# Tile starts, one moved recombination unit, one moved split and two re-divided copies in a two-layer encoder

## The chip, the cores and the metric

The kernel runs on one core of one Trainium2 chip. The metric is device time in microseconds of one execution. A core has five engines that run side by side, each with its own queue of instructions in a fixed order: TensorE (PE in the profile; PEld is its loading of stationary operands), VectorE (DVE), ScalarE (ACT), GpSimd (POOL) and SyncE (SP), which here issues the loads of the weights. They wait for each other through semaphores. SBUF is the on-chip memory (128 partitions), PSUM the memory into which TensorE accumulates.

## The reference

An encoder trunk of two layers in float32, for one sequence of 256 tokens with 2048 features. Each sub-layer is normalised in front and added to its input:

```
h = x
h = h + mixer_a(rms_norm(h, g0), w_a, w_ao, ...)   # grouped-query attention: 16 heads, 4 key/value heads
h = h + ffn(rms_norm(h, g1), w_up, conv, w_down)   # gated, a width-3 depthwise convolution between
h = h + mixer_b(rms_norm(h, g2), w_b, w_bo, bias)  # 3 groups of 8 heads: windows (128,1), (512,4), (2048,16)
h = h + ffn(rms_norm(h, g3), w_up, conv, w_down)
out = rms_norm(h, g4)
```

The FFN's inner width is 5632, computed in 11 pairs of 512 columns. Mixer B's attention output has 3072 features, so its output projection w_bo contracts 3072 rows, six chunks of 512.

## The kernel before

**Arithmetic.** Every projection in float32 is made of three matmuls in a reduced format: an operand x is split in a high part xh and the rest xl, a weight in wh and wl, and xh·wh, xh·wl and xl·wh are added in PSUM (L126 to L128). The weights come from memory as raw tiles of 128 x 2 x 512 floats (512 KB). ScalarE makes wh from raw (L138; in the units L173), VectorE makes wl = raw - wh (L139; L174), with four buffers of each.

**Feeds and units.** `feed` is one chunk (512 rows of contraction) for one block of 512 output columns and both halves of the tokens: 24 matmuls, which need two wh. `fast_unit` does one chunk for two column blocks with a seven-product scheme: 42 matmuls where two feeds would take 48, on seven weight tiles, some of which are sums of raw tiles (VectorE, L172). It needs recombined stationary operands: s and sx in mixer A's output projection, kTh, kTl, qTh, qTl in mixer B's; these are tiles that had another use before. Its products lie in eight accumulators of PSUM; after the last unit `fold` brings the shared ones together on VectorE (L193 to L203).

**The order of the work.** `pair` runs a list of feeds and units for two column blocks. Beside the matmuls run Python generators whose steps are taken between the matmuls of a feed or a unit (`step`): the bringing over of results to the next stage, the fold, the attention's arithmetic. So the order in which a step is issued is written out by the code, while a scheduler puts each engine's instructions in a final order, with wh and wl given a priority of 60 places ahead. In the end each engine works its list strictly in order.

**The border between two stages.** When the two accumulators of a block of 512 columns are complete, VectorE adds them to h (L452), ScalarE takes the sum of squares (L359), and `late_transpose` turns the block for the next projection: two transposes of 32 x 32 blocks on VectorE (L369) into quad, then 16 copies of 32 x 256 elements into wide, the even ones on GpSimd (L390) and the odd ones on ScalarE (L388), in two halves, each followed by a `yield`; then four `put`, which scale and split into xh and xl of the next stage (ScalarE L323, VectorE L326). For the last block (n=3) the copies are divided over three engines: GpSimd by `quad_move` (L373), ScalarE (L418), VectorE (L421). The FFN that follows takes its chunks in order, so the block n=2 is its third chunk.

**Mixer B.** The projection of values and gates runs while probabilities are turned and placed in the wide tiles kTh, kTl, qTh, qTl (n = 0 to 3; `place` in the value stage), for the two halves of the heads one after the other (hf = 0, 1). Each placing is `quad_move`: 16 copies on GpSimd (L373). Small matmuls with the values (L1265, ps<-wide,v) use them as soon as they are there. The output projection then does column blocks 0 and 1 with feeds alone, and blocks 2 and 3 with units for chunks 0 and 2 and feeds for chunks 1, 3, 4, 5.

**Memory.** Tiles come from pools in the order of their first use in the code, so the byte at which a tile begins in a partition depends on what was taken before it.

Of the kernel before, what the change touches and what calls it, by code (L numbers as in the profile page):

```python
# [7 lines left out]
F32 = mybir.dt.float32  # L8
F32R = mybir.dt.float32r
# [4 lines left out]
P = 128  # L14
# [16 lines left out]
def tile_encoder(ctx: ExitStack, tc: tile.TileContext, x, xT, w_a, w_ao, q_gain, k_gain, w_b, w_bo,  # L31
# [7 lines left out]
    small = ctx.enter_context(tc.tile_pool(name="small", bufs=2))  # L39
# [10 lines left out]
    nc.scalar.activation(act0, nhalf, AF.Copy)  # L50
    nc.gpsimd.dma_start(ident, ident_c)
    h = hpool.tile([P, 2, D], F32, name="h")

    uid = [0]

    def nm(s):
        uid[0] += 1
        return f"{s}_{uid[0]}"
# [30 lines left out]
    def drain(keep=0):  # L89
        while len(pending) > keep or beside:  # L90
            step(True)
            if len(pending) > keep:
                step()
# [111 lines left out]
    def pair(wd, ns, lhs, order, spot, folds, post, hurry=0, ready=None):  # L205
        (a2, a4), (a3, a8) = new_acc(), new_acc()
        acc, begun = {2: a2, 3: a3, 4: a4, 8: a8}, set()
        sides = [a2, a4], [a3, a8]
        fasts = [kg for kg, side in order if side is None]

        added = []

        def finish(side):
            add_residual(sides[side], ns[side])
            added.append(side)

        def closing():
            yield from fold(acc, *ns, *folds())
            for side in range(2 if post else 0):
                yield  # L220
                while side not in added:
                    yield
                post(ns[side])

        for i, (kg, side) in enumerate(order):
            while ready is not None and kg not in ready:
                step()
            if side is None:
                if kg == fasts[0]:
                    while beside:  # L230
                        step(True)
                    while ready is not None and "u" not in ready:
                        step()
                    acc.update({q: ps_tile() for q in (1, 5, 6, 7)})
                later = {s for _, s in order[i + 1:]}
                end = [q for q, s in ((1, None), (5, None), (6, None), (7, None), (2, 0), (4, 0), (3, 1))
                       if not later & {None, s}]
                fast_unit(acc, lhs[-1 - kg], wd[ns[0], kg], wd[ns[1], kg], begun, end, spot)
                if kg == fasts[-1]:
                    beside.append(closing())  # L240
                    if 0 not in later:
                        finish(0)
                continue
            mine = ((2, 4), (3, 8))[side]
            end = not any(s in (side, None) for _, s in order[i + 1:])
            feed(sides[side], lhs, kg, wd[ns[side], kg], not begun.issuperset(mine), end,
                 begun=[m for m in range(2) if mine[m] in begun])
            begun.update(mine)
            for _ in range(hurry):
                if pending:  # L250
                    step()
            if end:
                finish(side)
# [108 lines left out]
    def quad_tile(pool, tag, bufs=1):  # L362
        return pool.tile([P, 4, 8, 32], F32, tag=tag, name=nm("quad"), bufs=bufs)

    def wide_tile(pool, tag, bufs=1):
        return pool.tile([P, 8, P], F32, tag=tag, name=nm("wide"), bufs=bufs)
# [4 lines left out]
    def quad_move(o, quad, qcs=QC):  # L371
        for q, c in qcs:
            nc.gpsimd.tensor_copy(o[32 * c:32 * c + 32, :, 32 * q:32 * q + 32],  # L373
                                  quad[32 * q:32 * q + 32, c])
# [8 lines left out]
    def quad_place(o, quad, i0, i1):  # L383
        for i in range(i0, i1):
            q, c = QC[i]
            dst, src = o[32 * c:32 * c + 32, :, 32 * q:32 * q + 32], quad[32 * q:32 * q + 32, c]
            if i % 2:
                nc.scalar.activation(dst, src, AF.Copy)  # L388
            else:
                nc.gpsimd.tensor_copy(dst, src)  # L390

    def late_transpose(hT, n, g, pool, tag, new_quad):
        def put(kt, src):
            hT[kt] = new_hT(kt)
            split_scaled(*hT[kt][:2], src, gain[:, g, kt:kt + 1])

        yield
        if n < 3:
            quad = new_quad()
            for m in range(2):  # L400
                quad_T(quad, slice(m, 8, 2), h[:, m, n * 512:(n + 1) * 512])
            yield
            o = wide_tile(pool, tag)
            for i in range(0, 16, 8):
                quad_place(o, quad, i, i + 8)
                yield
            for j in range(4):
                put(4 * n + j, o[:, 2 * j:2 * j + 2].rearrange("p m c -> p (m c)"))
            return
        space, quad_tag, wide_tag = next_space[0]  # L410
        src = h[:, :, n * 512:(n + 1) * 512]
        quad, o = quad_tile(space, *quad_tag), wide_tile(space, *wide_tag)
        for m in range(2):
            quad_T(quad, slice(m, 8, 2), src[:, m])
        quad_move(o, quad, BY_POOL)
        yield
        for q, c in BY_ACT:
            nc.scalar.activation(o[32 * c:32 * c + 32, :, 32 * q:32 * q + 32], quad[32 * q:32 * q + 32, c], AF.Copy)  # L418
        for q, c in BY_DVE:
            rows, cols = slice(32 * q, 32 * q + 32), slice(32 * c, 32 * c + 32)  # L420
            nc.vector.transpose(o[cols, :, rows].rearrange("p (j m) t -> p j m t", m=2),  # L421
                                src[rows].rearrange("p m (j c) -> p j m c", c=P)[:, :, :, cols])
        yield
        yield
        for j in range(4):
            if j % 2 == 0:
                yield
            put(4 * n + j, o[:, 2 * j:2 * j + 2].rearrange("p m c -> p (m c)"))
# [54 lines left out]
    def ffn(l, hT, ss_in, cw, g_next, last, side=None):  # L483
        with tc.tile_pool(name=nm("fpool"), bufs=1) as fp:
            junk = junk_of(fp)
            next_space[0] = fp, ("quad", 2), ("cv", 1)
            drain(1)
            step()
            rstd = finish_rstd(ss_in)
# [148 lines left out]
            for hf, (p0, p1) in enumerate(HALVES):  # L638
                slots = {}
                ready.clear()  # L640
                new_us()
                fast = (1, 2)
                last_value = None
                for p in range(p0, p1):
                    k0 = 4 * (p - p0)
                    slots.update(new_slots(range(k0, k0 + 4)))
                    cg = fp.tile([P, 4, NT], F32, tag="cg", name=nm("cg"))
                    cv = fp.tile([P, 4, NT], F32, tag="cv", name=nm("cv"))
# [97 lines left out]
                both = {kg: [(kg, 0), (kg, 1)] for kg in rest}  # L746
                f0, f1 = ([(kg, None)] for kg in fast)
# [16 lines left out]
    def out_proj(w, slots, kgs, late, g_next, junk, pool, tag, new_quad, cuts=(), units=None):  # L764
        hTn, ss = {}, new_ss()

        def post(n):
            sumsq_cols(ss, n, junk)
            start(late_transpose(hTn, n, g_next, pool, tag, new_quad))

        def done(accs, n):
            add_residual(accs, n)
            post(n)

        if units:
            fast, own, tmp, spot, folds, raws = units
            done(project2(w, 0, 1, slots, kgs, late, lambda a: done(a, 0), None, cuts,
                          [lambda kg=kg: recombined(kg, slots, own, tmp) for kg in fast]), 1)
            extra[0] = raws
            both = {kg: [(kg, 0), (kg, 1)] for kg in sorted(kgs) if kg not in fast}  # L780
            (k0, k1, *ks), (f0, f1) = list(both), fast
            pair(w, (2, 3), slots, both[k0] + [(f0, None)] + both[k1] + [(f1, None)] + sum((both[k] for k in ks), []),
                 spot, folds, post)
            extra[0] = None
            drain(1)
            return hTn, ss
        done(project2(w, 0, 1, slots, kgs, late, lambda a: done(a, 0), None, cuts), 1)
        for n in (2, 3):
            done(project(w, n, slots, kgs), n)
        return hTn, ss  # L790
# [330 lines left out]
    def mixer_b(hT, ss_in):  # L1121
        with tc.tile_pool(name="bpool", bufs=1) as bp:
# [5 lines left out]
            slots = {}  # L1128
# [25 lines left out]
            for hf in range(2):  # L1154
# [61 lines left out]
                def value_stage(hf=hf, probs=probs, e=e, vs=vs):  # L1216
# [16 lines left out]

                    def place(quad, n):
                        o = wide_tile(bp, ("kTh", "kTl", "qTh", "qTl")[n])
                        quad_move(o, quad)
                        if n < 2:
                            for i in range(2):
                                turned[0, 2 * n + i] = o[:, 4 * i:4 * i + 4].rearrange("p x c -> p (x c)")
                        else:  # L1240
                            for i in range(4):
                                turned[n - 1, i] = o[:, 2 * i:2 * i + 2].rearrange("p x c -> p (x c)")
# [31 lines left out]
                    for n in range(2):  # L1274
                        quad = new_quad()
# [5 lines left out]
                    for n in (2, 3):  # L1281
                        i = 2 * (n - 2)
                        quad = new_quad()
# [138 lines left out]
```

## Time and profile before

| what | value |
| --- | --- |
| median of three runs | 2248.28 us (2247.81 to 2248.5) |
| profiled execution | 2248.33 us |
| its span | 2246.6 us |
| mean granted TensorE clock | 0.999 of full |
| TensorE busy | 2228.4 us (99%) |
| VectorE busy | 1718.7 us (77%) |
| ScalarE busy | 1313.3 us (58%) |
| GpSimd busy | 796.7 us (35%) |
| instructions | 28737 |

The span runs from the first to the last instruction of the profiled execution. In the views shown below a row of the timeline gives the start in us from the span's start, how long it lasted, the engine, the line of the code, the operation, the tile written and the tiles read, the shape, the number of like instructions in the row, and in brackets for how long the engine sat idle before it and what ended that. A row of the groups gives the count after the shape, then the total busy time and the mean ns of one. Matmuls overlap: one of 512 columns lasts about 390 ns, but the next starts some 227 ns after it. A tile's name stands without its buffer's number.

### The profile page before, as it was taken

What the parts mean: (1) busy time and instruction counts of PE and PEld (TensorE: products, weight loads), DVE (VectorE), ACT (ScalarE), POOL (GpSimd) and SP (SyncE); (2) the same over time, 40 slices, a digit from 0 to 9 for tenths busy, and PEclk for the clock granted to TensorE, in tenths of its full rate; (3) what the DMA queues carried; (4) which work ended last, traced back from release to release, by engine and by line L of the source; (5) the groups of instructions that cost most, each with busy time, mean ns of one, the idle gap of its engine ahead of it and who ended that gap; (6) DMA issues with size and microseconds to landing.
All of it is one profiled execution on the core that took longest, in us unless ns stands there. A gap on an engine that the chain in (4) does not pass through costs nothing.

```text
span 2246.6 us, 28737 instructions
## 1 busy us (share of the span) xinstructions
PE 2228.4 (99%) x10005; PEld 1842.9 (82%) x10005; DVE 1718.7 (77%) x2211; ACT 1313.3 (58%) x1842; POOL 796.7 (35%) x1051
## 2 busy tenths in 40 slices
PE   9999999999999999999999999999999999999998
PEld 7888888888888888888888888878888888888887
DVE  6877667778876788878877878686777798677795
ACT  7676655656545666755454554566665655465663
POOL 2343255661005563220062008013766500256601
PEclk9999999999999999999999999999999999999999
DMA  8665666565666565666666555556656566665653
GB/s 302 194 218 181 217 188 198 192 193 187 201 208 193 192 193 180 202 198 198 186 192 192 182 185 181 190 177 211 195 182 205 187 206 200 194 194 190 216 198 131
DMA packets 126178, 439.58 MB, mean 196 GB/s; under 512 B 14408, under 2 KB 18248, under 8 KB 126032
## 3 DMA queue, kind: packets, MB, share of 16 engines
q1 hardware_dynamic: 123056, 429.05, 59.0%
q0 software_dynamic: 2688, 8.39, 1.5%
q8 instruction: 78, 1.28, 0.2%
q14 instruction: 68, 0.56, 0.1%
q10 hardware_dynamic: 288, 0.30, 0.0%
HBM read 432.34 MB, written 5.34 MB: 195 GB/s over the span
## 4 chain that ended last, share of the span: by engine, by line
PE 83%; DVE 5%; POOL 1%; ACT 1%; issue 1%; DMA 1%; SPq 0%; POOLq 0%; DVEq 0%; ACTq 0%
PE acc L128 26%; PE acc L127 26%; PE acc L126 26%; DVE wl L174 1%; DVE wl L139 1%; PE ps L180 1%; PE ps L181 1%; PE ps L179 1%; PE acc L180 1%; PE acc L181 1%; PE acc L179 1%; POOL wide L390 1%; DVE cv L537 1%; POOL wide L373 1%; DVE u L172 0%
## 5 line engine op out<-in xcount | busy, mean ns | idle before, releaser
L139 DVE TENSOR_TENSOR wl<-raw,wh 128x1024 fp32r<-128x1024 f32 (+1 forms) x748 | 936.2, 1258 | 366.6 <-ACT wh L138 362.5
L138 ACT ACTIVATE wh<-raw 128x1024 fp32r<-128x1024 f32 (+1 forms) x748 | 782.8, 1050 | 658.4 <-PE acc L128 586.8
L126 PE MATMUL acc<-wh,xh 128*128 128x512 f32 x2176 | 848.3, 390 | 0.5 <-ACT wh L138 0.5
L127 PE MATMUL acc<-wl,xh 128*128 128x512 f32 x2176 | 847.3, 389 | 0.3 <-DVE wl L139 0.2
L128 PE MATMUL acc<-wh,xh 128*128 128x512 f32 x2176 | 847.2, 389 | 0.0
L550 POOL COPY u<-quad 32x256 f32<-32x256 f32 x672 | 483.1, 719 | 338.5 <-DVE quad L369 312.3
L128 PEld LDWEIGHTS acc<-wh,xh 128*128 128x128 f32 x2176 | 408.4, 188 | 85.0
L127 PEld LDWEIGHTS acc<-wl,xh 128*128 128x128 f32 x2176 | 408.7, 188 | 84.3 <-DVE wl L139 1.3
L126 PEld LDWEIGHTS acc<-wh,xh 128*128 128x128 f32 x2176 | 408.7, 188 | 84.3 <-ACT wh L138 0.9
L126 PE MATMUL acc<-wh,a 128*128 128x512 f32 x720 | 280.9, 390 | 0.0
L128 PE MATMUL acc<-wh,a 128*128 128x512 f32 x720 | 280.3, 390 | 0.0
L127 PE MATMUL acc<-wl,a 128*128 128x512 f32 x720 | 280.3, 389 | 0.0
L373 POOL COPY wide<-quad 32x256 f32<-32x256 f32 x165 | 111.1, 673 | 175.2 <-DVE quad L369 167.5
L128 PEld LDWEIGHTS acc<-wh,a 128*128 128x128 f32 x720 | 135.1, 188 | 28.4 <-DVE a L320 0.2
L126 PEld LDWEIGHTS acc<-wh,a 128*128 128x128 f32 x720 | 135.2, 188 | 27.8
L127 PEld LDWEIGHTS acc<-wl,a 128*128 128x128 f32 x720 | 135.2, 188 | 27.8
L390 POOL COPY wide<-quad 32x256 f32<-32x256 f32 x72 | 44.3, 615 | 207.1 <-DVE quad L369 193.2
L480 ACT ACTIVATE stg<-acc,rstd 128x512 f32<-128x512 f32 x122 | 82.9, 686 | 33.3 <-PE acc L128 33.2
L567 POOL TENSOR_TENSOR cv<-cg,cv 128x1024 f32<-128x1024 f32 x18 | 58.2, 3231 | 105.2 <-DVE cv L537 105.2
L173 ACT ACTIVATE wh<-raw 128x1024 fp32r<-128x1024 f32 x56 | 59.4, 1061 | 49.2 <-PE acc L128 44.3
L537 DVE SCALAR_TENSOR_TENSOR cg<-u,cw,cg 128x256 f32<-128x256 f32 x176 | 82.3, 511 | 4.5 <-ACT cg L529 4.5
L520 POOL MEMSET u<- 128x4 f32 x12 | 1.0, 107 | 231.8 <-DVE wl L174 211.9
(284 smaller groups left out, 2004.7 us busy)
## 6 DMA issues: line engine op xcount, KB each, us to landing
raw<-in_w_up_dram SPq DMA_DIRECT2D x352, 512.0 KB, 4.5
raw<-in_w_down_dram SPq DMA_DIRECT2D x176, 512.0 KB, 4.5
raw<-in_w_b_dram SPq DMA_DIRECT2D x144, 512.0 KB, 4.4
raw<-in_w_bo_dram SPq DMA_DIRECT2D x48, 512.0 KB, 4.2
raw<-in_w_a_dram SPq DMA_DIRECT2D x40, 512.0 KB, 4.7
raw<-in_w_ao_dram SPq DMA_DIRECT2D x32, 512.0 KB, 4.8
raw<-in_w_a_dram SPq DMA_DIRECT2D x16, 256.0 KB, 5.7
there<-quad POOLq DMA_DIRECT2D x6, 512.0 KB, 4.6
```

The lines of the kernel that those rows point to most:

```text
L126: nc.tensor.matmul(accs[m], xh, wh[:, j, :], start=st, stop=False)
L127: nc.tensor.matmul(accs[m], xh, wl[:, j, :], start=False, stop=False)
L128: nc.tensor.matmul(accs[m], xl, wh[:, j, :], start=False, stop=sp)
L138: nc.scalar.activation(wh[:, c], r[:, c], AF.Copy)
L139: nc.vector.tensor_tensor(wl[:, c], r[:, c], wh[:, c].bitcast(F32), ALU.subtract)
L173: nc.scalar.activation(wh, r, AF.Copy)
L373: nc.gpsimd.tensor_copy(o[32 * c:32 * c + 32, :, 32 * q:32 * q + 32], quad[32 * q:32 * q + 32, c])
L390: nc.gpsimd.tensor_copy(dst, src)
L480: nc.scalar.activation(o[:, m, :], accs[m], AF.Copy, scale=rstd[:, m:m + 1])
L537: nc.vector.scalar_tensor_tensor(cj, halves(flat[:, j, o:o + NT])[:, ::-1], tap(n, j, i), cj, ALU.mult, ALU.add)
L550: nc.gpsimd.tensor_copy(o, src)
L567: made.append(eng.tensor_tensor(cv, cg, cv, ALU.mult).ins)
```

## The change

There are four edits.

1. A tile of 32 bytes per partition, `space`, that nothing uses, is taken before the later pools; and in `ffn` the tiles quad (two buffers), cv and sx (two buffers) are taken when the pool opens instead of at their first use. Both move the bytes at which tiles begin.
2. In `late_transpose`, for the blocks n < 3, one more `yield` stands between the copies and the four `put`: the splits are issued one step later.
3. In mixer B's output projection, the order list of column blocks 2 and 3: each unit comes one chunk (two feeds, 48 matmuls) later. Before it was chunk 1, unit of chunk 0, chunk 3, unit of chunk 2, chunks 4 and 5; now it is chunks 1 and 3, unit of 0, chunk 4, unit of 2, chunk 5. The loads that SP issues follow that order.
4. In mixer B's `place`, for the second half of the heads and n = 2 and 3, `quad_place` stands in place of `quad_move`: 8 of the 16 copies go to ScalarE.

The number of matmuls is the same; GpSimd has 16 copies less, ScalarE 16 more.

```diff
@@ -50,6 +50,7 @@
     h = hpool.tile([P, 2, D], F32, name="h")
+    small.tile([P, 8], F32, name="space", bufs=1)
@@ -404,6 +405,7 @@
             for i in range(0, 16, 8):
                 quad_place(o, quad, i, i + 8)
                 yield
+            yield
             for j in range(4):
                 put(4 * n + j, o[:, 2 * j:2 * j + 2].rearrange("p m c -> p (m c)"))
             return
@@ -484,6 +486,9 @@
             next_space[0] = fp, ("quad", 2), ("cv", 1)
+            quad_tile(fp, "quad", 2)
+            wide_tile(fp, "cv")
+            fp.tile([P, 6, 2, P], F32R, tag="sx", name=nm("sx"), bufs=2)
             drain(1)
@@ -778,8 +783,8 @@
             both = {kg: [(kg, 0), (kg, 1)] for kg in sorted(kgs) if kg not in fast}
-            (k0, k1, *ks), (f0, f1) = list(both), fast
-            pair(w, (2, 3), slots, both[k0] + [(f0, None)] + both[k1] + [(f1, None)] + sum((both[k] for k in ks), []),
+            (k0, k1, k2, k3), (f0, f1) = both, fast
+            pair(w, (2, 3), slots, both[k0] + both[k1] + [(f0, None)] + both[k2] + [(f1, None)] + both[k3],
                  spot, folds, post)
@@ -1233,7 +1238,10 @@
                         o = wide_tile(bp, ("kTh", "kTl", "qTh", "qTl")[n])
-                        quad_move(o, quad)
+                        if hf == 1 and n > 1:
+                            quad_place(o, quad, 0, 16)
+                        else:
+                            quad_move(o, quad)
```

What that does to the engines' lists shows at three places. The rows name line, operation, tile written and tiles read, with buffer numbers; the lines after the change are one or two higher than before for the same code. First, ScalarE in mixer B's output projection, where the splits of block 1 (xh<-wide) meet the first unit's weights (L173 before, L174 after). Before:

```order
L173 ACTIVATE wh_12939<-raw_12928 128x1024
L388 ACTIVATE wide_12859<-quad_12840 32x8x32 x6
L173 ACTIVATE wh_12949<-raw_12930 128x1024
L388 ACTIVATE wide_12859<-quad_12840 32x8x32 x2
L323 ACTIVATE xh_12912<-wide_12859,gain 128x256
L323 ACTIVATE xh_12915<-wide_12859,gain 128x256
L323 ACTIVATE xh_12918<-wide_12859,gain 128x256
L173 ACTIVATE wh_12959<-raw_12932 128x1024
```

And after, the same copies and splits with weights of feeds (L139) among and behind them:

```order
L139 ACTIVATE wh_12920<-raw_12916 128x1024
L389 ACTIVATE wide_12863<-quad_12844 32x8x32 x6
L139 ACTIVATE wh_12948<-raw_12918 128x1024
L389 ACTIVATE wide_12863<-quad_12844 32x8x32 x2
L324 ACTIVATE xh_12936<-wide_12863,gain 128x256
L324 ACTIVATE xh_12939<-wide_12863,gain 128x256
L324 ACTIVATE xh_12942<-wide_12863,gain 128x256
L139 ACTIVATE wh_12968<-raw_12964 128x1024
L324 ACTIVATE xh_12945<-wide_12863,gain 128x256
L139 ACTIVATE wh_12984<-raw_12966 128x1024
L174 ACTIVATE wh_13015<-raw_13004 128x1024
```

The unit's weights have moved behind the splits and behind the weights of feeds. Second, GpSimd from the second half of the heads in mixer B on. Before:

```order
L373 COPY wide_11854<-quad_11845 32x8x32 x16
L373 COPY wide_11896<-quad_11887 32x8x32 x16
L373 COPY wide_12106<-quad_12061 32x8x32 x16
L373 COPY wide_12228<-quad_12183 32x8x32 x16
L390 COPY wide_12745<-quad_12726 32x8x32 x8
```

After:

```order
L374 COPY wide_11858<-quad_11849 32x8x32 x16
L374 COPY wide_11900<-quad_11891 32x8x32 x16
L391 COPY wide_12110<-quad_12065 32x8x32 x8
L391 COPY wide_12232<-quad_12187 32x8x32 x8
L391 COPY wide_12749<-quad_12730 32x8x32 x8
```

The third and the fourth tile keep eight copies on GpSimd; the other eight of each stand on ScalarE's list (L389). Third, VectorE ahead of the second FFN, where block 2's accumulators are added to h (L452 before, L454 after) and turned (L369, L370). Before, the fold is far ahead of it:

```order
L139 TENSOR_TENSOR wl_13274<-raw_13253,wh_13273 128x1024
L203 TENSOR_TENSOR h<-h,fold_13184 128x512
L139 TENSOR_TENSOR wl_13296<-raw_13291,wh_13295 128x1024
L139 TENSOR_TENSOR wl_13319<-raw_13293,wh_13318 128x1024
L139 TENSOR_TENSOR wl_13420<-raw_13415,wh_13419 128x1024
L452 TENSOR_TENSOR h<-acc_12816,h 128x512
L452 TENSOR_TENSOR h<-acc_12817,h 128x512
L369 STREAM_TRANSPOSE quad_13315<-h 128x16x32 x2
L139 TENSOR_TENSOR wl_13436<-raw_13417,wh_13435 128x1024
```

After:

```order
L195 TENSOR_TENSOR fold_13261<-ps_13003,fold_13260 128x512
L197 TENSOR_TENSOR fold_13261<-ps_13001,fold_13260 128x512
L140 TENSOR_TENSOR wl_13427<-raw_13422,wh_13426 128x1024
L454 TENSOR_TENSOR h<-acc_12808,h 128x512
L454 TENSOR_TENSOR h<-acc_12809,h 128x512
L198 TENSOR_TENSOR fold_13260<-ps_13001,fold_13261 128x512
L200 TENSOR_TENSOR h<-h,fold_13260 128x512
L201 TENSOR_TENSOR h<-h,fold_13261 128x512
L370 STREAM_TRANSPOSE quad_13341<-h 128x16x32 x2
L140 TENSOR_TENSOR wl_13443<-raw_13424,wh_13442 128x1024
```

Three adds of the fold now stand between the adds to h and the transposes.

## The prediction

> **What bounds the kernel now.** I read the page first, then TensorE's waits, then the matmuls one by one around each wait.
>
> ```profile
> span 2246.6 us, 28737 instructions
> PE 2228.4 (99%) x10005; PEld 1842.9 (82%) x10005; DVE 1718.7 (77%) x2211; ACT 1313.3 (58%) x1842; POOL 796.7 (35%) x1051
> PEclk9999999999999999999999999999999999999999
> ```
>
> TensorE is busy 99% of the span at full clock, so a change gains only where TensorE waits or where its matmuls are set further apart than they need be. The other engines matter through the moment at which they hand an operand over. The waits (total us, times, longest):
>
> ```profile
> PE ps L180 <- DVE wl L174: 2.2, 5, 0.7
> PE ps L335 <- DVE qTl L320: 1.9, 1, 1.9
> PE ps L1265 <- POOL wide L373: 1.7, 2, 1.2
> ```
>
> Two of these stand where the code changes: the probability tiles of mixer B (L1265) and the unit's weights (L180). The profiled execution took 2248.33 us, 1.7 more than its span and within 0.05 of the median (2248.28), so I sum against 2248.33. A measurement of this kernel can tell about 0.2%, 4.5 us, from no change: the bounds are 2243.8 and 2252.8.
>
> **Part 1: the starts of the operands.** The built programs show where each SBUF tile begins. Before, wh, wl, xh, a, s and c begin 64 bytes past a multiple of 128; sx begins at 0 and kTh, kTl, qTh, qTl at 32. Afterwards all of these are at 64. Inside one unit of mixer A's output projection both cases stand side by side:
>
> ```profile
> 902.35 0.40 PE L179 MATMUL ps<-wh,sx 128*128 128x512 f32 x1
> ...
> 905.15 0.39 PE L179 MATMUL acc<-wh,s 128*128 128x512 f32 x1
> ...
> 906.54 0.39 PE L179 MATMUL ps<-wh,s 128*128 128x512 f32 x1
> ...
> 910.62 0.40 PE L179 MATMUL acc<-wh,sx 128*128 128x512 f32 x1
> ```
>
> From 902.35 to 905.15 twelve matmuls with sx start, one every 233.3 ns; from 906.54 to 910.62 eighteen with s, one every 226.7. Same weights, same unit, nothing waited for: 6.6 ns apart. The groups by form show the same difference over the whole span (mean ns in the middle):
>
> ```profile
> L179 PE MATMUL ps<-wh,s 128*128 128x512 f32 x72 | 28.0, 390 | 0.0
> L179 PE MATMUL ps<-wh,sx 128*128 128x512 f32 x24 | 9.5, 396 | 0.0
> L127 PE MATMUL acc<-wl,sx 128*128 128x512 f32 x48 | 19.0, 396 | 0.0
> L127 PE MATMUL acc<-wl,c 128*128 128x512 f32 x16 | 6.3, 395 | 0.0
> L181 PE MATMUL ps<-wh,kTl 128*128 128x512 f32 x6 | 2.4, 395 | 0.0
> ```
>
> There are 360 matmuls with sx in all such groups: 360 x 6.6 ns = 2.4 us. The neighbours that overlap them (48 with c and 72 with s, at about half the excess) give 0.4, and 48 with kT or qT at 5 to 6 ns 0.3. Some 80 groups of mixer B's small attention products, whose operands also begin at 32 beside ones at 64, should give about 0.9; their rows have no twin at equal starts, so 0.9 is an estimate by the same excess per matmul that overlaps one of another start. I take 4.0. Ends: 0, if the start is not the cause, and 5.0, if the attention products gain twice that.
>
> Trainium skill, "SBUF — State Buffer", section "Who interferes with whom": TensorE has one read port for the moving and an independent one for the stationary operand, and never waits on anyone. By that rule where the operands start can cost nothing, and this term would be 0. The spacing above speaks against it as far as a difference in start can be told from a difference in tile; that is the first rival.
>
> **Part 2: two probability tiles moved by ScalarE too.** For the second half of the heads, tiles n=2 and 3 get 8 copies on GpSimd and 8 on ScalarE where GpSimd made 16.
>
> ```profile
> 1390.25 0.39 PE L128 MATMUL acc<-wh,a 128*128 128x512 f32 x1
> 1391.85 0.82 PE L1265 MATMUL ps<-wide,v 128*128 128x128 f32 x5 [1.22 <-POOL wide L373]
> ```
> ```profile
> 1378.03 24.52 POOL L373 COPY wide<-quad 32x256 f32<-32x256 f32 x32 [2.90 <-DVE quad L369]
> ```
> ```profile
> L388 ACT ACTIVATE wide<-quad x72: 413/416/419, 213.4 to 1525.5; 32x256 f32<-32x256 f32 x72
> ```
> ```profile
> L390 POOL COPY wide<-quad x72: 392/396/1302, 212.8 to 1526.1; 32x256 f32<-32x256 f32 x72
> ```
> ```profile
> 1381.11 1.06 ACT L138 ACTIVATE wh<-raw 128x1024 fp32r<-128x1024 f32 x1 [1.65 <-PE acc L128]
> ```
>
> GpSimd needs 24.52 us for 32 copies, 12.3 a tile, and TensorE comes 1.2 us too early for the first and 0.5 for the second. With half the copies a GpSimd share is about 6.1 us, and ScalarE's 8 x 0.416 = 3.3 run beside it: the tile is ready some 5 to 6 us sooner, far more than 1.2. Gain: both L1265 waits, 1.7, and the restart behind each, 0.15 (1391.85 - 1390.25 - 0.23 = 1.37 lost for a wait of 1.22): 2.0. Ends: 0, if ScalarE's share comes late, and 2.0, since no more is lost there. What ScalarE's 16 copies push back are the wh copies of the projection that runs meanwhile. Each feeds 12 matmuls, 2.7 us, and there are four buffers, so a wh is wanted 3 x 2.7 = 8.2 us after its buffer is freed; ScalarE idles for that buffer (1.65). A block of 3.3, the copy of 1.06 and VectorE's split of 1.25 are 5.7: hidden, with 2.5 over. If ScalarE were to take both blocks at once, 6.7 + 2.3 = 9.0 would show by 0.8.
>
> **Part 3: border splits one step later, units one chunk later.** The order of the engines at other borders stays but for one pair of VectorE adds: nothing, hidden by the feeds there, bounds minus and plus 0.1. At the end of mixer B:
>
> ```profile
> 1472.34 0.39 PE L181 MATMUL acc<-wh,a 128*128 128x512 f32 x1
> 1473.59 0.51 PE L179 MATMUL acc<-wh,kTh 128*128 128x512 f32 x1 [0.85 <-ACT wh L173]
> 1474.85 0.50 PE L180 MATMUL acc<-wl,kTh 128*128 128x512 f32 x1 [0.76 <-DVE wl L174]
> ...
> 1476.11 0.40 PE L179 MATMUL ps<-wh,kTh 128*128 128x512 f32 x1
> 1477.17 0.50 PE L180 MATMUL ps<-wl,kTh 128*128 128x512 f32 x1 [0.66 <-DVE wl L174]
> ...
> 1496.20 0.39 PE L179 MATMUL acc<-wh,qTh 128*128 128x512 f32 x1
> 1496.69 0.50 PE L180 MATMUL acc<-wl,qTh 128*128 128x512 f32 x1
> ```
> ```profile
> 1471.28 1.31 ACT L323 ACTIVATE xh<-wide,gain 128x256 fp32r<-128x256 f32 x3 [3.80 <-POOL wide L390]
> 1472.49 1.04 ACT L173 ACTIVATE wh<-raw 128x1024 fp32r<-128x1024 f32 x1
> ```
> ```profile
> 1462.47 8.77 POOL L390 COPY wide<-quad 32x256 f32<-32x256 f32 x8 [10.01 <-DVE quad L369]
> ```
>
> Less the normal 0.23, the first unit loses 1.02, 1.03 and 0.83 there, and 0.1 for each of the two restarted matmuls that take 0.50: 3.1. The second loses 0.26 + 0.1 = 0.4. The cause is ScalarE's order: three xh splits wait 3.80 for GpSimd's slow 8.77 us of copies, with the unit's wh behind them, and a unit uses up a wh every six matmuls, 1.36 us. Afterwards four feed wh's, wanted 2.7 us apart, stand between those copies and the unit, which comes 48 matmuls, 10.9 us, later, so ScalarE is ahead again when it begins. Gain 3.0, nearest to the second unit, which has no xh ahead of it and loses 0.4 where the first loses 3.1. Ends: 0, if the wait only changes its place (a feed's wh held up by 3.8 + 1.06 + 1.25 = 6.1, under 8.2), and 3.4, both units' losses. The unit's four loads stand behind four more on SP's queue but are used as much later: nothing, bounds 0 and 0.4, the second unit's present loss.
>
> The price is at the FFN's start. Now four feeds lie between the second unit and the FFN:
>
> ```profile
> 1503.52 0.39 PE L126 MATMUL acc<-wh,a 128*128 128x512 f32 x1
> ...
> 1525.28 0.39 PE L126 MATMUL acc<-wh,xh 128*128 128x512 f32 x1
> ```
> ```profile
> 1509.77 0.68 DVE L197 TENSOR_TENSOR fold<-ps,fold 128x512 f32<-128x512 f32 x1
> 1519.55 1.28 DVE L452 TENSOR_TENSOR h<-acc,h 128x512 f32<-128x512 f32 x2
> ...
> 1529.18 1.24 DVE L326 SCALAR_TENSOR_TENSOR xh<-wide,gain,xh 128x256 fp32r<-128x256 f32 x3
> 1530.33 0.70 DVE L369 STREAM_TRANSPOSE quad<-h 128x512 f32<-128x512 f32 x1
> 1530.96 1.18 DVE L139 TENSOR_TENSOR wl<-raw,wh 128x1024 fp32r<-128x1024 f32 x1
> ```
> ```profile
> 1522.20 4.27 POOL L390 COPY wide<-quad 32x256 f32<-32x256 f32 x8 [50.95 <-DVE quad L369]
> ```
>
> 21.76 us hold 96 matmuls (0.2267 each); afterwards 48, 10.9 us, and the fold's adds move into the stretch where columns 2 are added to h, turned (GpSimd, 4.27) and split for the FFN. The adds at 1519.55 wait for accumulators, 5.7 us before the FFN in both programs; but three fold adds (3 x 0.68 = 2.0) and a sum of squares with one wh on ScalarE (0.8 more) now come between them and the copies: 2.8 later. The wl at 1530.96 is done at 1532.1 and wanted three wh's into the FFN, at 1525.28 + 3 x 2.72 + 0.23 = 1533.7: 1.5 to spare. The transpose of 1530.33 goes ahead of the splits, 0.6 back. So 2.8 - 0.6 - 1.5 = 0.7 of wait and 0.1 of restart: a loss of 0.8. Ends: 0, if ScalarE catches up, and 5.1 (second rival).
>
> **Sum.** -4.0 - 2.0 - 3.0 + 0.8 = -8.2; 2248.33 - 8.2 = 2240.1.
>
> **The rivals.**
> - The start is not the cause of the 6.6 ns: part 1 gives 0 and the time is 2244.1. For it: sx differs from s in more than its start. Against: kT, qT, c and sx, written by different instructions, all show 395 or 396 ns. By the Trainium skill's rule on the ports, above, this rival would be the outcome.
> - The border's chain stays as long behind the second unit as it is: from 1503.52 to the splits' end at 1530.4, 26.9 us (25.1 by the first split). Afterwards it is wanted 10.9 + 10.9 = 21.8 after that unit: a wait of 3.3 to 5.1 instead of 0.8, 2242.6 to 2244.4. Against: 16 of those us are a wait for the accumulators of 1519.55, which now end sooner after the unit.
> - ScalarE's share of a probability tile is queued behind wh copies and the L1265 waits stay: 2242.1. Against: a wh copy is only 1.06.
> - The other side, slower. GpSimd's copies at the FFN's start run at their slowest, 1.302 instead of 4.27/8 = 0.53 each: +6.1 on the 26.9 chain, 33.0, a wait of 11.2 at one place. So long a wait could drop the clock, as at the launch, where eleven matmuls take 5.06 us:
>
> ```profile
> 1.45 5.06 PE L440 MATMUL ps<-warm 128*128 128x512 f32 x11 [1.45 <-DVE warm L437]
> ```
>
> Their starts are (5.06 - 0.65)/10 = 0.44 apart, so fifteen slow ones add 15 x 0.21 = 3.2. Together 14.4, against gains of 9.0: 2253.7. It cancels the gain from a wait of 9.0 on and is slower by over 0.2% from 13.5 with its clock loss. Against: the 8.77 us row is the slowest group near here, and no wait now exceeds 1.9. That a longer idle stretch halves the clock is a rule of the Trainium skill ("TensorE: Matmul & The Clock Gate", Part 1); no run here shows it behind a wait.
>
> **How the numbers follow.** Forecast 0.70; start not the cause 0.12; long chain 0.09; ScalarE late 0.03; slower 0.06. The forecast's own range is 2237.5 to 2242.5 (0.5 more from alignment and nothing lost at the FFN below; 2.4 lost in part above). For eight in ten I go from 2237.0 to 2244.2, which reaches the first two rivals. Faster: 0.70 + 0.03 + 0.06 of the long chain = 0.79. Within 0.2%: the 0.12, whose 2244.1 lies just above the bound, and the rest of the long chain, 0.15. Slower 0.06.
>
> **What would show it.** Right: groups with sx, c, kT and qT at 389 to 390 ns; no L1265 wait on GpSimd; L388 with 88 copies and L373 with 133; no wait on wh in the first unit; at most a wait under 1 us on a wl at mixer B's FFN. Wrong: sx still at 395, or neighbours that get slower; a wait of several us at that FFN's start; new waits on wh around the probability tiles; a granted clock under 0.999.

## The result and the profile after

The changed kernel takes 2240.71 us (median of six runs, 2239.19 to 2241.6) against 2248.39 (2247.81 to 2249.14): a ratio of 0.9964 with a 95% interval of 0.9952 to 0.9977, or 7.7 us less. The forecast was 2240.1, 8.2 less.

The page of the profile after:

```profile
span 2239.8 us, 28736 instructions
PE 2225.2 (99%) x10005; PEld 1843.6 (82%) x10005; DVE 1719.6 (77%) x2211; ACT 1320.1 (59%) x1858; POOL 784.2 (35%) x1035
```

TensorE's waits after (total us, times, longest):

```profile
PE ps L336 <- DVE qTl L321: 2.0, 1, 2.0
PE ps L181 <- DVE wl L175: 1.6, 4, 0.4
PE ps L442 <- DVE warm L439: 1.5, 1, 1.5
PE acc L128 <- DVE wl L140: 1.2, 3, 0.6
PE acc L127 <- ACT wh L139: 0.7, 1, 0.7
```

The waits for GpSimd at the probability tiles and for wh and wl at mixer B's units are gone. What remains of L181 are four waits of 0.4 in the FFNs, which were there before as well.

The profiled execution of after took 2241.6, the slowest of its six. To see where the time went, the matmuls can be matched: both kernels have 10005 matmul records, and away from the units that were moved the same number is the same matmul. The table gives the us between the starts of nine such matmuls, the first row from the span's start, in the profiled executions of before, after and four of the experiments told of below (e8 carries all four edits and one more):

| stretch | before | after | e1 starts | e2 copies | e3 units | e8 order |
| --- | --- | --- | --- | --- | --- | --- |
| mixer A, first 213 us | 213.03 | 213.94 | 213.48 | 212.87 | 213.98 | 213.33 |
| to the last unit of the first FFN (911 us) | 698.53 | 698.03 | 697.97 | 698.53 | 698.60 | 697.96 |
| rest of that FFN, mixer B to 1375 us | 463.49 | 462.81 | 463.00 | 463.58 | 463.87 | 462.88 |
| probability tiles, second half of the heads | 45.15 | 43.04 | 44.91 | 43.06 | 45.12 | 43.04 |
| next 45 us | 44.88 | 44.88 | 44.88 | 44.88 | 44.88 | 44.88 |
| units and feeds to the second FFN | 60.19 | 56.44 | 60.69 | 60.93 | 56.76 | 56.44 |
| first 65 matmuls of that FFN | 14.73 | 15.34 | 14.73 | 14.73 | 15.37 | 14.73 |
| second FFN, to its last unit | 636.11 | 635.46 | 635.70 | 636.15 | 636.13 | 635.39 |
| last 62 us | 62.62 | 62.06 | 62.08 | 62.65 | 62.62 | 62.10 |

Behind mixer A's first 213 us, where the edits change nothing but the bytes at which some tiles begin and which differ by 1 us among these executions, the gain is 7.6: the eight lower rows of before sum to 2025.7, those of after to 2018.1. The copies, the units and the loss stand in rows of their own; the starts are spread over the others.

The operands: groups by form of after, which answer to those at 395 and 396 ns before, and one of the small attention products (pTl,vh).

```profile
L128 PE MATMUL acc<-wl,sx 128*128 128x512 f32 x48 | 18.7, 389 | 0.0
L180 PE MATMUL ps<-wh,sx 128*128 128x512 f32 x24 | 9.3, 389 | 0.0
L335 PE MATMUL ps<-pTl,vh 128*128 128x256 f32 x32 | 9.1, 283 | 0.0
L128 PE MATMUL acc<-wl,c 128*128 128x512 f32 x16 | 6.2, 389 | 0.0
L182 PE MATMUL ps<-wh,kTl 128*128 128x512 f32 x6 | 2.3, 389 | 0.0
```

The probability tiles: TensorE, GpSimd and ScalarE of after.

```profile
1390.17 0.39 PE L129 MATMUL acc<-wh,a 128*128 128x512 f32 x1
1390.40 1.05 PE L1273 MATMUL ps<-wide,v 128*128 128x128 f32 x8
```
```profile
1377.76 5.90 POOL L391 COPY wide<-quad 32x256 f32<-32x256 f32 x8 [2.90 <-DVE quad L370]
1389.21 6.29 POOL L391 COPY wide<-quad 32x256 f32<-32x256 f32 x8 [5.56 <-DVE quad L370]
```
```profile
1389.12 3.41 ACT L389 ACTIVATE wide<-quad 32x256 f32<-32x256 f32 x8 [0.17 <-DVE quad L370]
```

GpSimd's half of the first tile is ready at 1383.7 (1377.76 + 5.90) and TensorE comes at 1390.4, 0.23 behind the matmul ahead of it: nothing is lost.

The first unit of mixer B begins (L180) 0.22 behind the last feed, and ScalarE has its wh ready long before:

```profile
1478.12 0.39 PE L129 MATMUL acc<-wh,a 128*128 128x512 f32 x1
1478.34 0.39 PE L180 MATMUL ps<-wh,a 128*128 128x512 f32 x1
```
```profile
1467.36 0.49 ACT L324 ACTIVATE xh<-wide,gain 128x256 fp32r<-128x256 f32 x1
1467.75 1.05 ACT L139 ACTIVATE wh<-raw 128x1024 fp32r<-128x1024 f32 x1
1470.38 1.06 ACT L174 ACTIVATE wh<-raw 128x1024 fp32r<-128x1024 f32 x1 [1.58 <-PE acc L129]
```

ScalarE waits for a free buffer there (1.58), where it had made TensorE wait before. The price is at the second FFN's start, on TensorE and VectorE:

```profile
1527.30 0.39 PE L127 MATMUL acc<-wh,xh 128*128 128x512 f32 x1
1527.98 0.50 PE L128 MATMUL acc<-wl,xh 128*128 128x512 f32 x1 [0.29 <-DVE wl L140]
```
```profile
1525.52 1.27 DVE L327 SCALAR_TENSOR_TENSOR xh<-wide,gain,xh 128x256 fp32r<-128x256 f32 x3
1526.71 1.22 DVE L140 TENSOR_TENSOR wl<-raw,wh 128x1024 fp32r<-128x1024 f32 x1
```

The wl stands behind three splits of block 2 and is done at 1527.93; TensorE starts 0.68 after the matmul ahead instead of 0.23, and the restarted one takes 0.50: 0.45 and 0.11, the 0.6 of the table.

### The profile page after: what moved, and what is told of

It reads as the page before. It is cut to its first block, busy times and chain, and to the rows that moved or that the text cites. A ratio compares the mean times of both kernels' runs of the same rounds, so it can differ in the third digit from the quotient of the medians.

```text
span 2239.8 us, 28736 instructions
## 1 busy us (share of the span) xinstructions
PE 2225.2 (99%) x10005; PEld 1843.6 (82%) x10005; DVE 1719.6 (77%) x2211; ACT 1320.1 (59%) x1858; POOL 784.2 (35%) x1035
## 4 chain that ended last, share of the span: by engine, by line
PE 90%; DVE 6%; issue 1%; ACT 1%; POOL 1%; DMA 1%; SPq 0%; DVEq 0%; POOLq 0%; ACTq 0%
PE acc L129 28%; PE acc L128 28%; PE acc L127 28%; DVE wl L175 2%; DVE wl L140 1%; DVE u L173 1%; PE ps L181 1%; PE ps L182 1%; PE ps L180 1%; DMA raw<-in_w_a_dram 1%; PE acc L181 1%; PE acc L182 1%; PE acc L180 1%; DVE cv L542 1%; ACT wh L139 0%
## 5 line engine op out<-in xcount | busy, mean ns | idle before, releaser
L139 ACT ACTIVATE wh<-raw 128x1024 fp32r<-128x1024 f32 (+1 forms) x748 | 782.6, 1049 | 643.8 <-PE acc L129 572.5
L374 POOL COPY wide<-quad 32x256 f32<-32x256 f32 x133 | 89.1, 670 | 169.3 <-DVE quad L370 159.8
L391 POOL COPY wide<-quad 32x256 f32<-32x256 f32 x88 | 53.3, 605 | 223.4 <-DVE quad L370 155.7
L174 ACT ACTIVATE wh<-raw 128x1024 fp32r<-128x1024 f32 x56 | 59.5, 1062 | 53.7 <-PE acc L129 48.9
```

The lines of the kernel that those rows point to most:

```text
L139: nc.scalar.activation(wh[:, c], r[:, c], AF.Copy)
L174: nc.scalar.activation(wh, r, AF.Copy)
```

## The experiments

Two theories were held against each other. By the prediction's, three separate losses were removed (distance of the operands' starts, GpSimd's copies, ScalarE's order at the units) and one small wait was bought. By its rivals, one of them is not the cause or moves elsewhere.

### Each part alone

**e1: edit 1 alone on the kernel before.**

```diff
+    small.tile([P, 8], F32, name="space", bufs=1)
...
+            quad_tile(fp, "quad", 2)
+            wide_tile(fp, "cv")
+            fp.tile([P, 6, 2, P], F32R, tag="sx", name=nm("sx"), bufs=2)
```

> Edit 1 alone on the kernel before. If two operands of a matmul that begin at different places of a 128-byte line set matmuls further apart (A): groups with sx, kT and qT at 389 to 390 ns instead of 395 to 396, the waits at the probability tiles and at mixer B's units as before, and 3 to 4 us less, about 2245. If the start is not the cause (B): sx still at 396 and no change.

Measured: ratio 0.9988 (0.9979 to 0.9997), median 2245.72. The groups with sx are at 389 and 390 where nothing is waited for, and the waits at the probability tiles and in the first unit stay, at 1.2 instead of 1.7 for the tiles:

```profile
PE ps L1269 <- POOL wide L374: 1.2, 2, 0.7
PE acc L180 <- ACT wh L174: 0.8, 1, 0.8
PE acc L181 <- DVE wl L175: 0.8, 1, 0.8
```

In the table, the five rows behind 213 us without the units' and the two that stay equal lose 0.56, 0.49, 0.24, 0.41 and 0.54: 2.2 us; the units' row hides its 0.3 (after less e3) behind a drop of the clock, told of below. So the edit is worth 2.5 to 2.7. The starts are a cause; that the size was below the 3 to 4 expected is taken up below.

**e2: edit 4 alone.**

```diff
-                        quad_move(o, quad)
+                        if hf == 1 and n > 1:
+                            quad_place(o, quad, 0, 16)
+                        else:
+                            quad_move(o, quad)
```

> Edit 4 alone. If the two waits on GpSimd's copies are a cost of their own: both gone, sx still at 396, the units' waits as before, 2.0 to 2.2 us less, about 2246.2. If ScalarE's share only comes late in its place: a wait for ScalarE there of a like size and no change.

Measured: 0.9990 (0.9981 to 0.9999), median 2246.5. The row of the tiles loses 2.09 and no wait at L1265 or for ScalarE is left there. The units' row is 0.7 longer: a wl of the second unit came later, and its matmul starts 1.16 after the one ahead (at 1494.11), where it was 0.49 before:

```profile
1495.27 0.50 PE L180 MATMUL acc<-wl,qTh 128*128 128x512 f32 x1 [0.77 <-DVE wl L174]
```

That is 100 us behind the edit, at a place with no slack. The traces show what came late: VectorE's first sum for that unit waits for a weight tile to land, before and in e2:

```profile
1488.47 1.22 DVE L172 TENSOR_TENSOR sum<-raw,raw 128x1024 f32<-128x1024 f32 x1 [3.01 <-DMA raw<-in_w_bo_dram]
```
```profile
1487.05 1.23 DVE L172 TENSOR_TENSOR sum<-raw,raw 128x1024 f32<-128x1024 f32 x1 [3.66 <-DMA raw<-in_w_bo_dram]
```

VectorE works on from that sum to the late wl without a gap. In e2 the matmul ahead of the wait comes 2.09 sooner (1494.11, before 1496.20) and the sum only 1.42, so the weights are 0.67 nearer to their use. Why the load did not land sooner by as much is open, and one trace does not tell whether it is so each time. With edit 3 as well nothing is waited for there.

**e3: edits 2 and 3 together.** The `yield` of edit 2 and the order list of edit 3.

> Edits 2 and 3 together, without 1 and 4. If the order of ScalarE's list is the cause: no wait in either unit (3.4 us less), a wait of about 0.5 us on a wl at the FFN behind mixer B, about 2245.5. If a shortage of buffers or loads were the cause, the first unit keeps about 3 us of waits in its new place: about 2248.8.

Measured: 0.9988 (0.9979 to 0.9996), median 2246.17. The units' row loses 3.43, the start of the FFN gains 0.64 of wait: both as expected from ScalarE's order; the expected 0.5 was a little low. The three ratios' gains add to 0.34% against 0.36% for the whole change: no interplay that the runs could show.

**e7: edit 3 alone, and e10: edit 2 alone.**

> Edit 3 alone (units later, the splits where they were). If the units' place does the work: no wait in the first unit, 3.0 to 3.4 us of waits gone there, and a wait of 0.3 to 0.6 us on a wl at the FFN behind mixer B, as with edits 2 and 3 together. If the later splits do it: the first unit's waits stay.

> Edit 2 alone (the splits one step later). ScalarE's list is the same as before, so if that list is the cause the units' waits of 3.4 us stay and no wait on a wl appears at the FFN. If the later splits did the work in the pair of edits: the first unit's waits go.

Measured, one run each: 2245.83 and 2251.58, beside 2248.97 for the kernel before. By the matched matmuls e7 takes 56.76 in the units' row and 15.35 at the FFN's start, the same as e3; e10 takes 60.36 and 14.73, the same as before within 0.2. In e10 the units' waits stand as they were:

```profile
PE acc L180 <- DVE wl L174: 1.0, 2, 0.8
PE acc L179 <- ACT wh L173: 0.9, 1, 0.9
```

So the units' place does all of it and the later splits nothing that can be seen there. Beside the trace of before, e10's is 3.2 us longer, and 2.6 of these lie in mixer A (215.62 in its first 213 us), ahead of everything that its edit touches.

**e8: the feeds in another order**, on the kernel after, to take the bought wait away:

```diff
-both[k0] + both[k1] + [(f0, None)] + both[k2] + [(f1, None)] + both[k3]
+both[k0] + both[k1] + [(f0, None), (k2, 0), (f1, None), (k3, 0), (k2, 1), (k3, 1)]
```

> The kernel after, with one change in the order of column blocks 2 and 3: the feed of chunk 5 for block 2 goes ahead of the feed of chunk 4 for block 3, one feed stands between the units and three behind the second, so block 2's accumulators end two feeds (10.9 us) ahead of the FFN and not one (5.4). If the wait on a wl at that FFN comes from block 2's chain: it is gone, 0.5 to 0.6 us less, about 2240.1, and only the trace can tell. If the units stand too close now: waits on wh or wl come back in the second unit, up to the 3.4 us of before.

Measured: 0.9965 (0.9952 to 0.9979), median 2241.35 beside 2249.62 for the kernel before. The trace shows 14.73 at the FFN's start, as before the change, and 56.44 in the units' row, as after: the wait is gone and none came back. The remaining waits for wh and wl of feeds are 0.5 and 0.2 in mixer A:

```profile
PE acc L127 <- ACT wh L139: 0.5, 1, 0.5
PE acc L128 <- DVE wl L140: 0.2, 1, 0.2
```

It confirms that block 2's chain was late. Behind mixer A it gains 8.3 us against before where the change gains 7.6; the times cannot tell the two apart.

### What the distance of the starts costs

In these runs nearly all moving and stationary operands are put at a chosen distance, by unused bytes ahead of a pool; on every engine the order of instructions is that of after.

**e4: weights' tiles 64 bytes on.**

```diff
+    spool.tile([P, 16], F32, name="shift", bufs=1)
     small.tile([P, 8], F32, name="space", bufs=1)
```

> The kernel after, with 64 unused bytes ahead of the weights' tiles: wh and wl now begin at 0 of a 128-byte line and so do sx, kT, qT; xh, a, s and c stay at 64. By A the roles change: some 9100 matmuls now have their two operands 64 bytes apart and take 6.6 ns more each, 60 us, about 2301, with sx at 389 to 390 and xh, a and s at 396. By B no change, about 2240.7.

Measured: 1.0036 (1.0023 to 1.0050), median 2257.3. The direction is right for both groups, the size is not:

```profile
L128 PE MATMUL acc<-wh,xh 128*128 128x512 f32 x2176 | 854.8, 393 | 0.0
L129 PE MATMUL acc<-wl,xh 128*128 128x512 f32 x2176 | 852.7, 392 | 0.2 <-DVE wl L141 0.2
L130 PE MATMUL acc<-wh,xh 128*128 128x512 f32 x2176 | 849.9, 391 | 0.0
L182 PE MATMUL ps<-wl,sx 128*128 128x512 f32 x24 | 9.4, 390 | 0.0
```

The matmuls with sx, whose distance is still 0, stay fast and those with xh become slow, so it is not the tile but the distance; but the loss is some 2.4 ns each from start to start (16.6 us in the median, against the change's 2240.71) and not 6.6. Theory A as stated, with a period of 128 bytes and one price, falls.

**e9: xh, a, s and c at 0, weights at 64.**

```diff
+    hpool.tile([P, 16], F32, name="shift")
+    spool.tile([P, 16], F32, name="back", bufs=1)
```

> The kernel after, with xh, a, s and c moved to 0 of a 128-byte line while wh and wl stay at 64 (sx, kT, qT at 64 too): the same pair of starts, stationary at 0 and moving at 64, that sx had before, now in some 9100 matmuls. If the size of the loss hangs on which of the two operands begins where (A1): 6.6 ns each, 60 us, about 2300. If it does not, and the 6.6 was something of sx itself (A2): 2.2 to 2.7 ns each as with the roles the other way round, about 2257.

Measured: 1.0038 (1.0024 to 1.0052), median 2257.93: the small loss again.

```profile
L130 PE MATMUL acc<-wl,xh 128*128 128x512 f32 x2176 | 854.4, 393 | 0.0
```

Counted modulo 512 bytes, e9 and e4 are the same: the moving operand begins 64 bytes past the stationary one (+64). In the kernel before, sx began on a multiple of 512 and the weights 64 bytes short of one: -64. So a theory C was formed: the signed distance modulo 512 counts. 512 bytes is one row, 128 float32, of a stationary operand of 128x128.

**e5: weights 32 bytes on** (as e4, with [P, 8]).

> The kernel after, with 32 unused bytes ahead of the weights' tiles: wh and wl at 96, sx, kT and qT at 96 too, xh, a, s and c at 64, so that the two operands lie 32 bytes apart in some 9100 matmuls. By A any difference of start costs: 2 to 6 ns each, 2259 to 2295. If only a distance of 64 costs: no change, about 2240.7.

Measured: one run, 2296.07 beside 2249.62 for the kernel before.

```profile
L129 PE MATMUL acc<-wl,xh 128*128 128x512 f32 x2176 | 859.8, 395 | 0.5 <-DVE wl L141 0.5
L182 PE MATMUL ps<-wl,sx 128*128 128x512 f32 x24 | 9.3, 389 | 0.0
```

At +32 the full 6 ns and more; from start to start it is 6.7 ns on the average of all matmuls with xh.

**e11: the pair of starts that sx had, in nearly all matmuls.** The pools of h and of the weights change places and 192 bytes go ahead of h.

```diff
-    hpool = ctx.enter_context(tc.tile_pool(name="hpool", bufs=1))
     spool = ctx.enter_context(tc.tile_pool(name="spool", bufs=1))
+    hpool = ctx.enter_context(tc.tile_pool(name="hpool", bufs=1))
...
+    hpool.tile([P, 48], F32, name="shift")
```

> The kernel after, with the pools of h and of the weights changed in place and 192 unused bytes ahead of h: wh and wl begin at 448 of a 512-byte line and xh, a, s and c at 0, the very pair of starts that sx had before (the moving operand 64 bytes ahead of a multiple of 512, the stationary on it). The two runs with 64 bytes had the moving operand 64 bytes past the stationary one, modulo 512. If the signed distance modulo 512 counts (C): 6.6 ns in some 9100 matmuls, 60 us, about 2300. If 64 bytes cost the same on both sides and sx was special (A2): 2.2 to 2.7 ns, about 2258.

Measured: one run, 2294.63.

```profile
L129 PE MATMUL acc<-wl,xh 128*128 128x512 f32 x2176 | 860.4, 395 | 0.1
```

At -64 the loss is 6.7 ns, at +64 it was a third of that. Theory C holds in its sign. (The few matmuls with sx, kT and qT lie 192 bytes short there; those with sx come some 4 ns late.)

**e12: weights 128 bytes on** (as e4, with [P, 32]).

> The kernel after, with 128 unused bytes ahead of the weights' tiles: wh and wl (and sx, kT, qT) 128 bytes past xh, a, s and c modulo 512, so the same place of a 128-byte line. If the period is 128 bytes (A): no change, about 2240.7. If it is longer (C): slower by some ns per matmul, 10 to 60 us.

Measured: one run, 2284.65.

```profile
L129 PE MATMUL acc<-wl,xh 128*128 128x512 f32 x2176 | 858.7, 395 | 0.3 <-DVE wl L141 0.2
```

At the same place of a 128-byte line, but 128 bytes apart, a matmul starts 5.7 ns late. The period is longer than 128.

**e6: everything behind h 64 bytes on**, so that all begin at 0 of a 128-byte line.

```diff
+    hpool.tile([P, 16], F32, name="shift")
```

> The kernel after, with everything behind h moved by 64 bytes: all the operands that began at 64 begin at 0. By A only the difference of the two starts counts: 226.7 ns as at 64, no change, about 2240.7. If 64 itself is the fast place: slower in all matmuls, 20 us or more.

Measured: 0.9966 (0.9954 to 0.9979), as the change itself.

```profile
L129 PE MATMUL acc<-wl,xh 128*128 128x512 f32 x2176 | 848.6, 390 | 1.3 <-DVE wl L141 1.2
```

Whether both begin at 0 or at 64 of a 128-byte line makes no difference, as long as they begin alike. Together, as the mean delay of the next matmul's start with xh over 226.6 ns, worked out from the starts in the traces (gaps over 245 ns left out):

| moving less stationary start, modulo 512 bytes | 0 (after) | 0 (e6) | +32 (e5) | +64 (e4) | +64 (e9) | +128 (e12) | -64 (e11) |
| --- | --- | --- | --- | --- | --- | --- | --- |
| ns per matmul | 0.3 | 0.3 | 6.7 | 2.4 | 2.4 | 5.7 | 6.7 |

That 512 is a full period follows from after itself: its xh tiles begin at 448 and at 960 of 1024, the weights at 960, and all are fast. Why +64 costs less than the others was not found, and what in the chip makes the distance count is not shown either.

## Why the prediction was right

**Which bound, and where.** Right: TensorE at 99% gains only by its waits and its spacing, and behind mixer A's first 213 us nothing else in the table moved.

**Part 1, starts.** Right in its cause, too high in size: 4.0 forecast, 2.5 to 2.7 measured. The step that failed is the 0.9 for mixer B's small attention products. Their rows read 283 ns after as before:

```profile
L334 PE MATMUL ps<-pTl,vh 128*128 128x256 f32 x32 | 9.1, 283 | 0.0
```

In the kernel before, both operands of these products began at 32; the prediction wrote that they stood beside ones at 64, which holds for their neighbours only, and priced those as if they were in the pair. The rest was 3.1 by the forecast. Matched one by one in before and after, the 360 matmuls with sx and their neighbours come 2.4 us closer together where 2.8 was forecast (from start to start 233.2 ns became 227.1, so 6.1 and not 6.6); the 0.3 in the units' row fits. The rule "equal modulo 128" was also too loose (e12); the change fulfils the stricter one, modulo 512, so the forecast was not hurt by it. One place was named wrongly, in the prediction and in the words on the kernel: the unit at 902 to 912 us and its tiles s, sx belong to the first FFN's down projection, not to mixer A's output projection. No number hangs on it.

The Trainium skill's page "SBUF — State Buffer", section "Who interferes with whom", gives TensorE one read port for each operand and says that it never waits on anyone. The first rival rested on the same thought. The trace does not agree: with nothing changed but the distance of the starts, matmuls came 0.3 or 6.7 ns late, and the kernel took 2242.5 (e6) or 2294.63 (e11). The measurement decides.

**Part 2, copies.** Right: 2.0 forecast, 2.1 measured, alone and with the rest. GpSimd's eight copies took 5.9 and 6.3 us (6.1 forecast), ScalarE's 3.41 (3.3), and no wh came late. L389 (L388 before) has 88 copies and L374 (L373) has 133, as the prediction said.

**Part 3, units.** Right in cause and place: 3.0 forecast, 3.4 measured, since the second unit's 0.4 went too; the prediction had kept it. The later splits, on which it put nothing, did nothing (e10). The bought wait was 0.8 by the forecast and 0.6 in the trace, on the wl behind three splits, as it said, and it goes with block 2's chain (e8). That small term is right partly by luck. GpSimd's copies there began 1.8 us later against the FFN's start (1519.14) than before, 1.3 ahead of it where it was 3.1, and not 2.8, and took 6.04 us where the prediction used 4.27; the wl was done 1.9 later against the FFN's start, where 2.2 was forecast:

```profile
1517.87 6.04 POOL L391 COPY wide<-quad 32x256 f32<-32x256 f32 x8 [53.42 <-ACT wh L139]
```

**The sum.** -2.7 - 2.1 - 3.4 + 0.6 = -7.6 by the table, -7.7 by the medians, -8.2 by the forecast. Errors of opposite sign bring the sums together: part 1 was forecast 1.3 too high, the other three terms together 0.7 too low. The rivals: the start is the cause (e1, e4); the long chain cost 0.6 and not 3.3 to 5.1; ScalarE's share was not late (e2); the slower side did not come, since no wait of after exceeds 2.0. One of the signs of being wrong did show, a granted clock under 0.999: 0.998 in one of the six runs. It tells nothing here, since the kernel before has 0.998 in seven of the ten runs beside e6.

## What to carry to other kernels

When TensorE is busy all the time, compare the mean duration of matmuls of one shape by their operands: a few ns between groups can mean that the moving and the stationary operand begin at different places of a 512-byte row, which here cost up to 6.7 ns of 227 in every matmul, 3% of it, and was mended by a few unused bytes. That was seen with matmuls of 128x512 in this one format; others were not tried. Work that strictly ordered engines do for another stage should not stand in front of the stretch that consumes fastest; moving the hungry stretch by one chunk was enough, and the trace, not the median, shows such gains of 2 to 3 us.

## What was not expected of the hardware

The granted clock halved for some 3.4 us behind the wait for qTl at 142 us, in mixer A, in some executions and not in others. TensorE's windows of after (us, then busy time of PE, PEld, DVE, ACT, POOL, the granted clock, the DMA share, GB/s):

```profile
144.00:146.00 2.00, 1.32 (x6) 1.22 (x7) 2.00 (x4) 0.00 (x0) 0.00 (x0) 0.73 0.66 201
146.00:148.00 2.00, 2.00 (x6) 1.61 (x5) 1.12 (x3) 0.68 (x3) 0.00 (x0) 0.50 0.96 286
148.00:150.00 2.00, 2.00 (x11) 1.64 (x11) 0.29 (x2) 1.47 (x3) 1.04 (x1) 0.92 0.91 272
```

The three windows lack 0.27, 0.50 and 0.08 of 2 us each, which makes 3.4 us at half the clock. Six matmuls there take 0.63 instead of 0.39 and start 0.43 apart; the sixteen matmuls behind the wait take 4.92 us where they took 3.32 in before, 1.6 more. The kernel before, with the same wait of 1.9, stayed at 1.00 in these windows; of the thirteen other profiled executions, after among them, seven show the drop, all behind a wait of 1.86 to 1.97, and two with waits of 1.94 and 1.95 (e10, e4) do not. In e1 a second drop stands behind the units' waits (0.84, 0.76 and 0.46); in before, with 0.85, 0.76 and 0.66 at the same place, the clock stayed at 1.00:

```profile
1476.00:1478.00 2.00, 1.68 (x4) 1.39 (x5) 2.00 (x4) 0.87 (x1) 0.00 (x0) 0.50 0.39 154
```

So removing a wait of one or two us may gain more than the wait, though no run here removes that of qTl. It does not explain the spread of mixer A's first 213 us: the three executions of the table with less than 213.4 are two with the drop (e2, e8) and one without (before). The Trainium skill, "TensorE: Matmul & The Clock Gate", Part 1, tells of half speed after an idle window of about 3.4 us and of windows that run freely, so that the same kernel differs from run to run; these traces show it behind waits of 1.9 us, and not each time.
